# Splitting each weight block once per layer and keeping both parts in HBM scratch

## The chip, the core and the metric

The kernel runs on one core of a Trainium2 chip. The metric is the device time of one execution in microseconds (us). Before the change it is 1161.77 us, the median of three runs (1158.14 to 1165.17).

## The reference

Two layers of a hybrid encoder run over nine tiles of 128 tokens: eight tiles of one prompt of 1024 tokens, and one tile with the 8 x 16 tokens of the sample requests. Both request groups use the same weights. Cut to what matters here:

```
h = x @ w_in                                     # 1024 x 3072
uA, vA, zA, qB, fB, iB, zB, qC, kC, vC, zC = split(h)
yA = sgu(uA, vA) * silu(zA)                      # gated mixing in chunks of 128
yB = norm(hgrn2(qB, fB, iB)) * silu(zB)          # gated recurrence, 4 heads
yC = window_attention(qC, kC, vC) * silu(zC)     # 8 query heads, 2 kv heads
out = layer_norm(alpha * x + concat(yA, yB, yC) @ w_out)   # 1024 x 1024
```

All of it is float32. The outputs are the last layer's rows, the new keys and values, the recurrent states and some normalised rows of the sample.

## The kernel before

**Numbers.** A large product is made of three passes of TensorE (PE) over operands that are each split in a high part (rounded to the format fp32r) and a low part (the remainder): high by high, then the two mixed products, all summed in one PSUM tile (`prod`, L336). So every weight is needed as `wh` and `wl`, and every activation as `xh` and `xl` (or `mixh` and `mixl`).

**Blocks.** The weights are cut in blocks of 1024 x 256: twelve of `w_in` and four of `w_out` per layer, 1 MB each. A block is used for three tiles of tokens. Either it makes three products of 24 matmuls with 256 columns (`tok_major`, L346; the blocks K, Q0, Q1, I, ZB, V and O0 to O3), or two products of 24 matmuls with 384 columns (`feat_major`, L353; F, Q, U, Z, C0, C1).

**Groups.** The nine tiles are worked on in groups of three (`GROUPS`, L45), layer by layer, so there are six groups, n = 0 to 5. Group n runs the twelve `w_in` blocks of its own layer and, between Q1 and the rest, the four `w_out` blocks of group n - 1. The last group's four `w_out` blocks end the program. That makes 96 blocks, and each of the 32 different blocks is loaded and split three times.

**Loading and splitting.** `issue_w` (L274) runs two blocks ahead of the block that PE works on. It takes a pair of buffers `wh`, `wl` (there are two pairs) and issues four loads of 256 KB into staging tiles `wst` (a ring of four; L286). Each loaded piece is then split: ScalarE (ACT) copies it to `wh` with rounding (`copy`, L125), and VectorE (DVE) or GpSimd (POOL) subtracts to get `wl` (`tt`, L142). Which of the two subtracts piece 0 to 3 of a block is read from a table by the block's position in the program:

```
WDVE = ((1, 2), (1, 3), (1, 2, 3), (1,), (1,), (1, 3))
```

Each entry holds for 16 blocks and lists the pieces of DVE; the others are POOL's. The three first blocks go to DVE whole (`WDVE0`). Because a `wh`, `wl` pair is written again two blocks later, the split of a block cannot begin before PE has finished the block two places ahead of it.

**Order of the work.** PE's order is written out by hand (`manual_schedule`): after each product `tick` (L331) puts in a step of the three lanes that do the rest: lane C is attention (L487), lane B the recurrence (`hpre` L608, `lane_b` L654), lane A the gated mixing (L833). The order on ACT, DVE, POOL and on SyncE's (SP) queue is made by a scheduler from priorities. All DMAs are issued on SP, which takes its list in order: a DMA that waits holds up those behind it. Layer norm (`out_norm`, L875) ends in a store of the tile's rows (L900 for layer 0, into the scratch tensor `x1`), and `load_x` (L376, L380) reads them back for the next layer.

Of the kernel before, what the change touches and what calls it, by code (L numbers as in the profile page):

```python
# [8 lines left out]
F32 = mybir.dt.float32  # L9
# [11 lines left out]
P = 128  # L21
CB = 256
# [2 lines left out]
RMS_EPS = 1e-6  # L25
TINY = float(2.0 ** -60)
NWST = 4
WDVE = ((1, 2), (1, 3), (1, 2, 3), (1,), (1,), (1, 3))
NB1 = 3
NC4 = 3  # L30
PPT = 1
# [1 line left out]
WDVE0 = (0, 1, 2, 3)  # L33
# [63 lines left out]
def body(ctx: ExitStack, tc: tile.TileContext, A, O, cst):  # L97
    nc = tc.nc
# [6 lines left out]
    dp = ctx.enter_context(tc.tile_pool(name="dp", bufs=1, space=DRAM))  # L105
# [3 lines left out]
    def T(tag, shape, bufs, dt=F32):  # L109
        uid[0] += 1  # L110
        return sp.tile(shape, dt, tag=tag, bufs=bufs, name=f"{tag}_{uid[0]}")
# [12 lines left out]
    def copy(o, i):  # L124
        return act.activation(o, i, AF.Copy)  # L125
# [3 lines left out]
    def acquire(tag, bufs, *writers):  # L129
        r = rings.setdefault(tag, [0, []])  # L130
        r[0] += 1
        k = r[0] - 1 - bufs
        if k >= 0:
            for w in writers:
                tc.add_manual_dep(w.ins, r[1][k].ins.name, mybir.DependencyInfo(
                    mybir.DependencyClass.NoSync, mybir.DependencyReason.SCHED_ONLY), reason="ring order")

    def release(tag, ins, n=1):
        rings[tag][1] += [ins] * n

    def tt(e, o, a, b, op):
        return e.tensor_tensor(o, a, b, op=op)  # L142
# [125 lines left out]
    wlist += [(order[-1][0], "w_out", cb) for cb in range(4)]  # L268
    wq = []
    wpos = [0]  # L270

    pieces = []

    def issue_w(off=WP):  # L274
        if wpos[0] >= len(wlist):
            return
        l, name, blk = wlist[wpos[0]]
        early = wpos[0] if wpos[0] < NEA else None
        eng_lo = WDVE0 if early is not None else WDVE[min(wpos[0] // 16, 5)]
        wpos[0] += 1  # L280
        with tc.high_priority(offset=off):
            wh, wl = T("wh", [P, 8, CB], 2, F32R), T("wl", [P, 8, CB], 2, F32R)
            for kk in range(4):
                tag, bufs = ("wst", NWST) if early is None or kk == 3 else ("pT", 3) if early % 2 == 0 else ("c4", NC4)
                st = T(tag, [P, 2, CB], bufs)
                ld = nc.sync.dma_start(st, A[name][l, :, blk, 2 * kk:2 * kk + 2, :])  # L286

                def piece(kk=kk, st=st, tag=tag, bufs=bufs, ld=ld):
                    hw, lw = wh[:, 2 * kk:2 * kk + 2, :], wl[:, 2 * kk:2 * kk + 2, :]
                    with tc.high_priority(offset=WP):  # L290
                        copy(hw, st)
                        up = tt(dve if kk in eng_lo else pool, lw, st, hw.bitcast(F32), ALU.subtract)
                    acquire(tag, bufs, ld)
                    release(tag, up)
                pieces.append(piece)
        wq.append((wh, wl))
# [5 lines left out]
    def next_w():  # L302
        do_pieces(99)
        w = wq.pop(0)
        issue_w()
        return w
# [601 lines left out]
    with tc.high_priority(offset=2 * WP):  # L908
        xrs = load_xT(GROUPS[0][:1], 2)
    issue_w(2 * WP - 100)  # L910
    with tc.high_priority(offset=2 * WP - 200):
        xrs += load_xT(GROUPS[0][1:])
# [234 lines left out]
```

## Time and profile before

| | before |
|---|---|
| median of the runs | 1161.77 us |
| the profiled execution | 1161.45 us |
| its span, first to last instruction | 1159.7 us |
| PE busy | 1097.3 us (95%) |
| PE's weight loads busy | 1015.6 us (88%) |
| DVE busy | 833.7 us (72%) |
| ACT busy | 628.6 us (54%) |
| POOL busy | 586.2 us (51%) |
| DMA: bytes, share of the 16 engines | 140.12 MB, 38% |
| mean granted TensorE clock | 0.973 |

The busy time of an engine is the time in which at least one of its instructions ran. Matmuls overlap in the pipeline, so PE's busy time is not its time at full rate. The granted clock is a share of 2.4 GHz. The page of the profile gives sums over the whole span; the windows view gives the same by stretch, and the timeline and the chain of waits tell what an engine stood still for.

### The profile page before, as it was taken

The page shows a single profiled execution, that of the slowest core. Times are in us where ns is not written, and L with a number is a line of the kernel's source. Part 1 is how long each engine was busy: PE and PEld are TensorE (multiplying, and loading weights), DVE is VectorE, ACT ScalarE, POOL GpSimd, SP SyncE. Part 2 cuts the span into 40 slices and gives each one's busy share as a digit, 9 for nine tenths or more (in the row PEclk, how much of TensorE's full clock was granted, in tenths as well). Part 3 has the DMA queues.
Part 4 walks back from the last instruction along what each step waited for, and adds up shares of the span by engine and source line. Part 5 has one row for each costly group of instructions (what it writes and reads, how often), then busy time and mean ns, then how long its engine had stood idle before and what let it go on. Part 6 is the DMA issues. An engine that isn't in the chain of part 4 may idle for free.

```text
span 1159.7 us, 26399 instructions
## 1 busy us (share of the span) xinstructions
PE 1097.3 (95%) x10267; PEld 1015.6 (88%) x10267; DVE 833.7 (72%) x1816; ACT 628.6 (54%) x1533; POOL 586.2 (51%) x634
## 2 busy tenths in 40 slices
PE   9989999999999999989999989999897999989886
PEld 7977799988889988989998978998897999888786
DVE  4688667785786787686777687477749658968965
ACT  5677545665444677444478554465644436554321
POOL 3344374262647235673336765536556461547523
PEclk9999999999999999999999999999999999989998
DMA  9322253253335334325236324324433432443231
GB/s 321 121 74 74 72 157 114 98 179 94 103 112 185 94 119 157 108 75 175 89 100 228 110 75 139 123 92 164 122 101 109 146 119 74 145 146 93 64 99 60
DMA packets 70093, 140.12 MB, mean 121 GB/s; under 512 B 8400, under 2 KB 11984, under 8 KB 69968
## 3 DMA queue, kind: packets, MB, share of 16 engines
q1 hardware_dynamic: 69968, 138.43, 37.7%
q8 instruction: 81, 1.33, 0.5%
q14 instruction: 44, 0.36, 0.1%
HBM read 126.87 MB, written 11.53 MB: 119 GB/s over the span
## 4 chain that ended last, share of the span: by engine, by line
PE 48%; DVE 14%; ACT 3%; POOL 3%; issue 2%; DMA 1%; POOLq 0%; SPq 0%; DVEq 0%; ACTq 0%
PE mm L344 38%; DVE wl L142 2%; PE ax L444 2%; DVE W L142 2%; PE ax L482 2%; PE ax L473 2%; DVE t1b L142 1%; ACT wh L125 1%; POOL sm L369 1%; PE ax L392 1%; POOL X L142 1%; DVE xrow L895 1%; PE ax L844 1%; PE ax L559 1%; DVE AQ L747 1%
## 5 line engine op out<-in xcount | busy, mean ns | idle before, releaser
L142 POOL TENSOR_TENSOR wl<-wst,wh 128x512 fp32r<-128x512 f32 x202 | 291.7, 1462 | 354.0 <-ACT wh L125 215.6
L142 DVE TENSOR_TENSOR wl<-wst,wh 128x512 fp32r<-128x512 f32 x173 | 197.5, 1163 | 116.9 <-ACT wh L125 112.1
L125 ACT ACTIVATE wh<-wst 128x512 fp32r<-128x512 f32 x375 | 206.9, 622 | 107.8 <-PE mm L344 89.5
L344 PE MATMUL mm<-wh,xh 128*128 128x256 f32 x864 | 129.1, 292 | 8.8 <-DVE t3k L364 5.9
L344 PE MATMUL mm<-xh,wh 128*128 128x384 f32 x576 | 127.0, 365 | 2.1 <-DVE t3k L364 1.3
L344 PEld LDWEIGHTS mm<-wh,xh 128*128 128x128 f32 x864 | 112.8, 194 | 14.9 <-DVE t3k L364 6.6
L344 PE MATMUL mm<-wh,xl 128*128 128x256 f32 x864 | 125.0, 288 | 0.0
L344 PE MATMUL mm<-wl,xh 128*128 128x256 f32 x864 | 123.3, 286 | 0.0
L344 PEld LDWEIGHTS mm<-wh,xl 128*128 128x128 f32 x864 | 114.6, 196 | 0.2 <-POOL xl L142 0.2
L344 PE MATMUL mm<-xl,wh 128*128 128x384 f32 x576 | 114.1, 340 | 0.0
L344 PEld LDWEIGHTS mm<-wl,xh 128*128 128x128 f32 x864 | 113.7, 195 | 0.0
L344 PEld LDWEIGHTS mm<-xh,wh 128*128 128x128 f32 x576 | 104.5, 201 | 9.0 <-issue 2.6
L344 PE MATMUL mm<-xh,wl 128*128 128x384 f32 x576 | 111.7, 335 | 0.0
L344 PEld LDWEIGHTS mm<-xl,wh 128*128 128x128 f32 x576 | 104.0, 193 | 0.0
L344 PEld LDWEIGHTS mm<-xh,wl 128*128 128x128 f32 x576 | 101.0, 188 | 0.0
L369 POOL TENSOR_TENSOR sm<-sm,ct 128x4 f32<-128x4 f32 (+2 forms) x42 | 48.7, 1159 | 82.7 <-DVE sm L368 75.6
L344 PE MATMUL mm<-wh,mixh 128*128 128x256 f32 x576 | 85.5, 291 | 4.9 <-ACT mixh L125 4.9
L344 PE MATMUL mm<-wh,mixl 128*128 128x256 f32 x576 | 82.4, 287 | 0.0
L458 ACT ACTIVATE c<-ax,sm 128x256 f32<-128x256 f32 (+1 forms) x128 | 57.4, 460 | 46.1 <-DVE sm L455 42.4
L344 PE MATMUL mm<-wl,mixh 128*128 128x256 f32 x576 | 81.8, 285 | 0.0
L344 PEld LDWEIGHTS mm<-wh,mixh 128*128 128x128 f32 x576 | 74.0, 191 | 5.3 <-ACT mixh L125 5.3
L344 PEld LDWEIGHTS mm<-wh,mixl 128*128 128x128 f32 x576 | 75.9, 196 | 0.0
(212 smaller groups left out, 1948.2 us busy)
## 6 DMA issues: line engine op xcount, KB each, us to landing
wst<-in_w_in SPq DMA_DIRECT2D x279, 256.0 KB, 3.1
wst<-in_w_out SPq DMA_DIRECT2D x96, 256.0 KB, 3.1
xrow<-x SPq DMA_DIRECT2D x18, 512.0 KB, 3.6
x<-xrow SPq DMA_DIRECT2D x9, 512.0 KB, 3.0
xrow<-in_xT SPq DMA_DIRECT2D x8, 512.0 KB, 4.6
xrow<-in_x_prompt SPq DMA_DIRECT2D x8, 512.0 KB, 3.5
out_y_prompt<-xrow SPq DMA_DIRECT2D x5, 512.0 KB, 3.6
pT<-in_w_in SPq DMA_DIRECT2D x6, 256.0 KB, 4.8
```

What stands on the lines that cost most here:

```text
L125: return act.activation(o, i, AF.Copy)
L142: return e.tensor_tensor(o, a, b, op=op)
L344: pe.matmul(out, a(k), b(k), start=n == 0, stop=n == 23)
L369: pool.tensor_tensor(out, out, mh[:, :out.shape[-1]], op=ALU.pow)
L392: pe.transpose(ps[:, k, :], xr[:, (4 * hf + k) * P:(4 * hf + k + 1) * P], idn)
L444: pe.matmul(ps[:, hh, sl], qT[:, hh, 2 * g + j, :], kk, start=hh + c == 0, stop=False)
L458: acquire("c4", NC4, *[act.activation(pt[:, h, sl], pss[h // 2][:, h % 2, sl], AF.Exp, bias=nM[:, h:h + 1], scale=0.125, accum_out=rs[:, h ...
L473: tr = pe.transpose(ps[:, h, :], pt[:, h, b * P:(b + 1) * P], idn)
L482: mm = pe.matmul(pso[64 * u:64 * u + 64], vv[:, g, :], pT[:, u::2, :], start=first, stop=last)
L559: mm = pe.matmul(pso[64 * u:64 * u + 64, b2, g].rearrange("p r i -> p (r i)"), w[:, 2 * p + b2, 64 * g:64 * g + 64], r[:, 64 * g + 32 * u: ...
L747: eng("v").tensor_copy(AQ[o, ch, u::2, :], QG[64 * u:64 * u + 64, :, 64 * ch:64 * ch + 64])
L844: pe.matmul(ps[64 * e:64 * e + 64, tl, :], v3[:, tl, gg * 64:(gg + 1) * 64], d["wsS" if m else "wsP"][:, gg, :], start=True, stop=True)
```

## The change

The first time that a layer's block comes up (groups 0 and 3 for `w_in`, groups 1 and 4 for `w_out`), it is loaded and split as before, and both parts are also written to scratch tensors in HBM, two pieces at a time, in DMAs of 512 KB. The second and third time the parts are read back straight into `wh` and `wl` by four DMAs of 512 KB; nothing is staged or split. The table of DVE's pieces now has one entry per layer: two of the four pieces of every block, after the first three.

```diff
-WDVE = ((1, 2), (1, 3), (1, 2, 3), (1,), (1,), (1, 3))
+WDVE = ((1, 3), (1, 3))
...
+    kept = {}
...
         early = wpos[0] if wpos[0] < NEA else None
-        eng_lo = WDVE0 if early is not None else WDVE[min(wpos[0] // 16, 5)]
+        eng_lo = WDVE0 if early is not None else WDVE[l]
         wpos[0] += 1
+        key = (l, name, blk)
         with tc.high_priority(offset=off):
             wh, wl = T("wh", [P, 8, CB], 2, F32R), T("wl", [P, 8, CB], 2, F32R)
+            if key in kept:
+                for h in range(2):
+                    ks = slice(4 * h, 4 * h + 4)
+                    nc.sync.dma_start(wh[:, ks, :].bitcast(F32), kept[key][0][:, ks, :])
+                    nc.sync.dma_start(wl[:, ks, :].bitcast(F32), kept[key][1][:, ks, :])
+                wq.append((wh, wl))
+                return
+            nm = f"{name}{l}_{blk}"
+            kept[key] = [dp.tile([P, 8, CB], F32, tag=nm + c, name=nm + c) for c in "hl"]
             for kk in range(4):
...
                     with tc.high_priority(offset=WP):
                         copy(hw, st)
                         up = tt(dve if kk in eng_lo else pool, lw, st, hw.bitcast(F32), ALU.subtract)
+                        if kk % 2:
+                            ks = slice(2 * kk - 2, 2 * kk + 2)
+                            nc.sync.dma_start(kept[key][0][:, ks, :], wh[:, ks, :].bitcast(F32))
+                            nc.sync.dma_start(kept[key][1][:, ks, :], wl[:, ks, :].bitcast(F32))
```

In the compiled program ACT's rounding copies fall from 384 to 128, DVE's subtractions for `wl` from 182 to 70, and POOL's from 202 to 58. The DMAs that stage weights fall from 384 to 128, and 128 writes and 256 reads of 512 KB are added. PE's instructions and their order stay as they were.

What moves is shown at three places. The first is SP's queue at the start, where the fourth piece of block I (`wst_372` before, `wst_392` after) waits its turn. `xrow` are the next group's tiles, `lng` and `lnb` the layer norm's parameters. Before:

```order
L286 DMA wst_370<-in_w_in 128x512
L208 DMA xrow_1976<-in_xT 128x1024
L208 DMA xrow_1978<-in_xT 128x1024
L224 DMA lng_2456<-in_ln_g 128x1024
L224 DMA lnb_2458<-in_ln_b 128x1024
L286 DMA wst_372<-in_w_in 128x512
L286 DMA wst_489<-in_w_in 128x512
```

After (`w_in_8h` and `w_in_8l` are the kept parts of block Q1, `w_in_5h` that of I):

```order
L208 DMA xrow_2046<-in_xT 128x1024
L208 DMA xrow_2048<-in_xT 128x1024
L224 DMA lng_2496<-in_ln_g 128x1024
L224 DMA lnb_2498<-in_ln_b 128x1024
L306 DMA w_in_8h<-wh_280 128x1024
L307 DMA w_in_8l<-wl_281 128x1024
L306 DMA w_in_8h<-wh_280 128x1024
L307 DMA w_in_8l<-wl_281 128x1024
L297 DMA wst_392<-in_w_in 128x512
L306 DMA w_in_5h<-wh_382 128x1024
```

The writes of Q1 now stand ahead of the last piece of I; the same four writes for K and for Q0 stand further up.

The second place is SP's queue in group 2, around the end of the `w_out` blocks, where the stores of the normalised rows (`x_91<-xrow`) and the next layer's loads of them lie between the weights of F, Q, U and I. Before, staged pieces:

```order
L286 DMA wst_5756<-in_w_in 128x512
L900 DMA x_91<-xrow_5006 128x1024
L380 DMA xrow_6912<-x_91 128x1024
L286 DMA wst_5850<-in_w_in 128x512
L286 DMA wst_5852<-in_w_in 128x512
```

After, the kept parts (4h is F, 3h is Q, 0h is U, 5h is I):

```order
L289 DMA wl_5403<-w_in_4l 128x1024 x2
L915 DMA x_91<-xrow_4912 128x1024
L288 DMA wh_5604<-w_in_3h 128x1024 x2
L289 DMA wl_5605<-w_in_3l 128x1024 x2
L395 DMA xrow_6676<-x_91 128x1024
L915 DMA x_91<-xrow_4914 128x1024
L915 DMA x_91<-xrow_4916 128x1024
L395 DMA xrow_6678<-x_91 128x1024
L288 DMA wh_5692<-w_in_0h 128x1024 x2
```

The reads of a block stand behind the stores of the rows and wait in the same queue for PE to release the buffer.

The third place is ACT's list at the end, from the last products of C1 (`tanh`) to the last layer norm. Before:

```order
L362 ACTIVATE tanh_14473<-mm_14448 128x384
L125 ACTIVATE mixh<-oT_12458 128x384
L125 ACTIVATE mixh<-u_1767_13196 128x384
L125 ACTIVATE wh_14543<-wst_14545 128x512
L125 ACTIVATE wh_14543<-wst_14547 128x512
L125 ACTIVATE wh_14543<-wst_14551 128x512
L125 ACTIVATE wh_14543<-wst_14549 128x512
L362 ACTIVATE tanh_14517<-mm_14492 128x384
```

After:

```order
L377 ACTIVATE tanh_13941<-mm_13916 128x384
L125 ACTIVATE mixh<-oT_12076 128x384
L125 ACTIVATE mixh<-u_1559_12766 128x384
L377 ACTIVATE tanh_13983<-mm_13958 128x384
L125 ACTIVATE mixh<-ax_13989 128x2x128
```

The four copies ahead of the last `tanh` are gone, as are the two subtractions ahead of its user on DVE.

## Rows read from the trace of the kernel before

**Rows 1.** The page's busy times: engine, us (share of the span), instructions.

```profile
PE 1097.3 (95%) x10267; PEld 1015.6 (88%) x10267; DVE 833.7 (72%) x1816; ACT 628.6 (54%) x1533; POOL 586.2 (51%) x634
```

**Rows 2.** Windows, groups 0 to 5, last four blocks: length, busy PE PEld DVE ACT POOL, clock, DMA, GB/s.

```profile
0.00:157.40 157.40, 145.91 (x1315) 130.65 (x1316) 107.51 (x265) 102.88 (x252) 69.34 (x85) 0.97 0.41 130
157.40:351.20 193.80, 186.84 (x1850) 172.26 (x1849) 144.93 (x312) 104.18 (x265) 93.93 (x98) 0.98 0.40 127
351.20:533.80 182.60, 178.73 (x1655) 166.19 (x1655) 131.45 (x279) 107.63 (x256) 97.22 (x121) 0.99 0.40 124
533.80:720.70 186.90, 179.22 (x1640) 167.35 (x1639) 137.41 (x294) 108.25 (x265) 100.12 (x94) 0.97 0.40 126
720.70:918.90 198.20, 189.43 (x1876) 175.90 (x1875) 135.16 (x302) 101.94 (x260) 108.54 (x116) 0.97 0.39 122
918.90:1108.40 189.50, 180.54 (x1656) 167.21 (x1655) 148.43 (x318) 94.04 (x223) 100.13 (x110) 0.97 0.35 111
1108.40:1150.00 41.60, 36.67 (x291) 36.10 (x289) 23.83 (x42) 8.53 (x17) 11.93 (x10) 0.96 0.19 61
```

**Rows 3.** Windows, same columns: a packed stretch, and one in which DMA is full.

```profile
400.00:440.00 40.00, 40.00 (x304) 35.90 (x303) 32.12 (x68) 31.59 (x90) 10.85 (x7) 1.00 0.38 130
...
24.00:26.00 2.00, 2.00 (x19) 2.00 (x18) 0.27 (x1) 0.38 (x1) 0.00 (x0) 1.00 1.02 417
```

**Rows 4.** Waits of PE: instruction, who it waited for, us in total, times, longest.

```profile
PE ax L827 <- DVE t1b L142: 16.6, 11, 2.9
PE mm L344 <- DVE t3k L364: 7.2, 5, 3.1
PE mm L344 <- ACT mixh L125: 4.9, 1, 4.9
...
PE mm L344 <- ACT wh L125: 1.5, 2, 1.3
```

**Rows 5.** The page's groups: the split; busy us, mean ns, idle before, releaser.

```profile
L142 POOL TENSOR_TENSOR wl<-wst,wh 128x512 fp32r<-128x512 f32 x202 | 291.7, 1462 | 354.0 <-ACT wh L125 215.6
L142 DVE TENSOR_TENSOR wl<-wst,wh 128x512 fp32r<-128x512 f32 x173 | 197.5, 1163 | 116.9 <-ACT wh L125 112.1
L125 ACT ACTIVATE wh<-wst 128x512 fp32r<-128x512 f32 x375 | 206.9, 622 | 107.8 <-PE mm L344 89.5
```

**Rows 6.** Timeline of POOL and DVE in group 4: start, us, instruction, count.

```profile
820.50 4.13 POOL L142 TENSOR_TENSOR wl<-wst,wh 128x512 fp32r<-128x512 f32 x3
...
887.47 0.89 DVE L142 TENSOR_TENSOR X<-X,t3k 128x128 f32<-128x128 f32 x4
```

**Rows 7.** The chain of waits in group 4 and at the first block of group 2.

```profile
821.98 3.76 DVE X L142 x5
...
351.49 8.62 PE mm L344 x72
```

**Rows 8.** Timeline at the last product of C1: ACT, DVE and PE.

```profile
1108.60 2.18 ACT L125 ACTIVATE wh<-wst 128x512 fp32r<-128x512 f32 x4
...
1109.77 3.02 DVE L142 TENSOR_TENSOR wl<-wst,wh 128x512 fp32r<-128x512 f32 x2 [0.48 <-ACT wh L125]
...
1114.66 0.58 PE L344 MATMUL mm<-wh,mixh 128*128 128x256 f32 x1 [4.93 <-ACT mixh L125]
```

**Rows 9.** DMA issues: form, count, KB each, median us from issue to landing.

```profile
xrow<-x SPq DMA_DIRECT2D x18, 512.0 KB, 3.6
x<-xrow SPq DMA_DIRECT2D x9, 512.0 KB, 3.0
```

**Rows 10.** Timeline of block I in group 0: its last split, and PE's start.

```profile
33.02 0.62 ACT L125 ACTIVATE wh<-wst 128x512 fp32r<-128x512 f32 x1
...
35.42 1.12 PE L344 MATMUL mm<-wh,xh 128*128 128x256 f32 x8
```

**Rows 11.** Timeline in group 2: a store on SP, and PE's start of block F.

```profile
425.56 0.33 SPq L900 DMA_DIRECT2D x<-xrow  x1
...
430.75 1.66 PE L344 MATMUL mm<-xh,wh 128*128 128x384 f32 x8
```

## The prediction

> **What bounds the kernel now.** I read the page's busy times first. PE is busy 1097.3 of 1159.7 us, the next engine 833.7 [rows 1]. So the question is how much of the remaining 62.4 us the change can reach. The windows tell where that is [rows 2]: PE's busy time falls short of the stretch by 11.5 us in group 0, 7.0, 3.9, 7.7, 8.8 and 9.0 us in groups 1 to 5, and 4.9 us in the last four blocks; most of the rest is the last layer norm. The same rows give the granted clock, 0.96 to 0.99 of full speed, so a little PE time is also lost to stretches at the lower of its two levels (1.2 and 2.4 GHz).
>
> That busy PE is really full shows in a packed stretch of attention and output blocks [rows 3]: 40 us of 40 at clock 1.00, no idle time at all, with PE's weight loads at 35.9 us, 90%. The Trainium skill ("Trainium Kernel Development and Optimization", Performance Expectations) says that matmul busy time is a bad metric and weight-load busy share a good one. By that share, 88%, some 12% or 140 us would be open; the packed row, where nothing is open at 90%, does not bear that out.
>
> What PE waits for is mostly not the weights. The direct wait for a rounded weight is 1.5 us in all; the long ones are results of DVE (t1b 16.6 us, t3k 7.2) and one of ACT (mixh 4.9) [rows 4]. These engines carry the split in their lists: 291.7 us on POOL, 197.5 on DVE, 206.9 on ACT, and the subtractions stand idle in the list besides, for 354.0 and 116.9 us, until a copy is done or PE releases the buffer [rows 5]. Whatever stands behind them waits too. So the split costs PE time by making the lanes late.
>
> **What the change takes away.** 64 of 96 blocks are read instead of split: 256 copies on ACT by 0.55 us (206.9/375) are 141 us, 112 subtractions on DVE by 1.163 are 130 us, 144 on POOL by 1.462 are 211 us [rows 5]. Nearly all of it leaves groups 1, 2, 4, 5 and the end. In these four groups DVE is busy 560 of 764 us and POOL 400 [rows 2]; about 123 and 202 us of that go, so DVE falls from 73% to 57% and POOL from 52% to 26%. DVE's other work also gets faster: while POOL ran three subtractions in 4.13 us, five small multiplications took DVE 3.76 us in the chain, 0.75 each; away from such pieces four of them took 0.89, 0.22 each [rows 6, 7].
>
> What can be won is bounded by PE's missing time there: 7.0 + 3.9 + 8.8 + 9.0 = 28.7 us, 4.9 us at the end, and the clock's share, (1 - clock) times the stretch, 3.9 + 1.8 + 5.9 + 5.7 + 1.7 = 19 us [rows 2]. Part of the lower clock lies in the idle time itself, so the ceiling is about 50 us. I take two thirds, 33 us: a queue's waits go about as busy over idle, 0.73/0.27 = 2.7 now and 0.57/0.43 = 1.3 after, which halves them, and the shorter operations beside POOL add to it. One place can be followed exactly. At the last product of C1 ACT does four copies (2.18 us) and DVE two subtractions (3.02 us) ahead of that product's own evacuation, and PE stands 4.93 us until mixh is there [rows 8]; with them gone some 4 us go. What is late next are the lanes' own chains, which is the third that I leave. Bounds: 17 us (only a third, the chains dominate) and 50.
>
> **What it adds at the start.** Each of the 32 split blocks writes 2.1 MB. In SP's order the fourth piece of block I now stands behind the twelve writes of K, Q0 and Q1, 6.29 MB. In the trace the queue is full then: 417 GB/s at share 1.02 [rows 3], so the writes push the piece back by 6.29/417 = 15.1 us. It was split at 33.02 us; now at about 48.1. PE starts I at 35.42 us and reaches the piece's rows with its seventh matmul of about 0.12 us, near 36.1 [rows 10]. That is a stall of about 12.5 us with the copy's 0.6; I take 12. The upper bound is the mean rate per share of group 0, 130/0.41 = 317 GB/s [rows 2]: 19.8 us, a stall of 17. The lower bound is 4: the lanes catch up meanwhile, and most of group 0's 11.5 us may be saved again. Behind I the order repeats (writes of a block, loads of the next), 3.1 MB per block or 7.5 us at 417 GB/s, under the 8.62 us that PE needs for a bare block [rows 7], so I put the rest of groups 0 and 3 at nothing; if the rate falls to 317 it is 9.9 us and each bare block there costs a little over 1. Twelve more of group 3's pieces go to DVE and twelve fewer to POOL; PE's idle time there is 7.7 us [rows 2], and I take 0 with bounds of 4 either way. A write waits on SP for its copy and its subtraction; behind it stand staging loads that wait for the same subtractions to free `wst`, so that wait is not new.
>
> **What the reads cost.** A read cannot start before PE releases the pair two blocks back, so it has the stay of one block on PE: 8.62 us at least [rows 7], 764/64 = 11.9 in the mean [rows 2]. One DMA of 512 KB lands 3.6 us after issue [rows 9]; three more at 417 GB/s take 1.26 us each, so a block is there after 7.4 us, and its first half, which is all that the first matmuls want, after less. That is hidden with 1.2 us to spare. The cover goes if the rate falls to 317 GB/s (8.6 us), or if SP is held. For the second I looked at the stores between the reads: in group 2 the first was issued at 425.56, and block F began on PE at 430.75 [rows 11], so the store is out of the queue at about the time that the next buffer is released. I take 0, with 20 us as the upper bound (two blocks of three tight ones in each of four groups late by 2 us, and the lower clock after each).
>
> **Sum.** Against the profiled execution's own 1161.45 us (0.3 under the median): -33 + 12 = -21, so 1140 us.
>
> **Rivals.** (a) The lanes' own chains are the limit and only 17 us come back: 1161.5 - 17 + 12 = 1156. For it: the direct waits on the split are small [rows 4]. Against: the slowed operations of rows 6 and 7, and the end of rows 8.
>
> (b) Slower: the reads come late. Before, staging ran a block ahead of the buffer; now one DMA stream must land within one block's stay. If a block takes 12 us to land (250 GB/s, 8.4 us, and a hold on SP), the half of the 64 blocks whose window lies between 8.62 and 11.9 us is late by 1.7 us in the mean, 54 us: 1161.5 + 54 + 12 - 33 = 1194. It decides from about 10.7 us on: with windows spread evenly from 8.62 to about 15 us, 64 x 2.1/6.4 = 21 blocks are then late by 1 us in the mean, which eats the net gain. For it: traffic grows from 140 to 274 MB. Against: 417 GB/s seen, and a mean share of only 0.35 to 0.41 per group [rows 2, 3]. The Trainium skill ("SBUF — State Buffer", the section on a bandwidth-pool intuition that's wrong) says that HBM is almost always the end-to-end bottleneck; by that rule the added 134 MB would come out on the span, at 417 GB/s some 320 us, and the shares of rows 2 say that it isn't so here.
>
> (c) Everything that PE misses comes back and the start is mostly absorbed: 1161.5 - 50 + 4 = 1115. For it: rows 6 to 8. Against: long chains of small operations in lane B stay.
>
> **Chances.** Forecast 0.58 (its own range 1126 to 1153), (a) 0.17, (b) 0.14, (c) 0.11. The range that leaves out two in ten goes from 1115, which takes in (c)'s point, to 1162, which takes in (a) and the upper bounds of start and reads. A measurement of this kernel can tell about 0.5% (6 us) from no change. Faster by more: the forecast, (c) and a third of (a), 0.74. Within it: most of (a), 0.10. Slower: (b) and the worst of (a), 0.16.
>
> **What would show it.** Right: ACT's copies near 70 us, DVE's subtractions near 80 and POOL's near 85; PE's idle time in groups 1, 2, 4, 5 together down from 28.7 to about 10 us; a wait of PE for the last piece of I near 36 us, about 12 us long; no wait of PE for a read of kept parts beyond 1 us; DMA share about 0.7. Wrong: PE waiting for DMAs into `wh` in block after block, which is (b); or the same t1b and t3k waits with DVE at 57%, which is (a).

## The result, and the profile after

The changed kernel takes 1126.71 us (median of four runs, 1125.85 to 1127.15); the kernel before took 1159.95 us beside it (1153.80 to 1165.17). The ratio is 0.9714, with a 95% interval of 0.9664 to 0.9765. The profiled execution of the change took 1125.85 us, with a span of 1124.1 us.

The page's busy times of the change, in the form of [rows 1]:

```profile
PE 1080.9 (96%) x10267; PEld 1003.2 (89%) x10267; DVE 652.5 (58%) x1704; ACT 503.8 (45%) x1277; POOL 367.8 (33%) x490
```

DVE lost 181 us, POOL 218 and ACT 125, while PE's instructions are the same. Of DVE's 181 us 136 are subtractions of the split (197.5 in [rows 5], 61.5 in the groups below); the other 45 come from operations that are the same in number and got shorter. Where it counts is seen in the windows by group (the columns of [rows 2]; the bounds are where the same products begin):

```profile
0.00:174.00 174.00, 149.73 (x1314) 135.49 (x1315) 100.92 (x263) 101.55 (x247) 65.56 (x83) 0.90 0.78 270
174.00:356.10 182.10, 181.96 (x1851) 168.71 (x1850) 106.86 (x289) 79.74 (x215) 56.09 (x73) 1.00 0.70 248
356.10:533.80 177.70, 176.98 (x1657) 164.57 (x1655) 91.59 (x234) 79.32 (x199) 65.93 (x105) 1.00 0.64 228
533.80:718.20 184.40, 177.57 (x1641) 165.58 (x1638) 122.94 (x295) 98.34 (x243) 71.21 (x73) 0.98 0.79 282
718.20:902.80 184.60, 184.48 (x1877) 171.40 (x1874) 108.94 (x295) 78.10 (x212) 51.59 (x75) 1.00 0.68 239
902.80:1077.90 175.10, 175.10 (x1656) 162.78 (x1654) 101.71 (x289) 63.61 (x160) 49.14 (x75) 1.00 0.63 216
1077.90:1114.30 36.40, 34.92 (x291) 34.63 (x288) 14.50 (x34) 1.89 (x4) 3.17 (x4) 1.00 0.53 183
```

Against the lengths in [rows 2], group 0 became 16.6 us longer, groups 1 to 5 became 11.7, 4.9, 2.5, 13.6 and 14.4 us shorter, and the last blocks 5.2: +16.6 - 52.3 = -35.7, which is the difference of the two spans (35.6). Groups 1, 2, 4 and 5 and the last blocks, where the prediction puts the relief, make 49.8 of the 52.3 us. In groups 1, 2, 4 and 5 PE now misses 0.14, 0.72, 0.12 and 0.00 us, 1.0 in all where it missed 28.7, and the granted clock there is 1.00. Group 3, which splits and writes like group 0, is 2.5 us shorter all the same.

The page's groups of what is left of the split, in the form of [rows 5]:

```profile
L142 POOL TENSOR_TENSOR wl<-wst,wh 128x512 fp32r<-128x512 f32 x58 | 84.6, 1472 | 210.2 <-ACT wh L125 126.2
L142 DVE TENSOR_TENSOR wl<-wst,wh 128x512 fp32r<-128x512 f32 x61 | 61.5, 1015 | 67.1 <-ACT wh L125 52.7
L125 ACT ACTIVATE wh<-wst 128x512 fp32r<-128x512 f32 x119 | 69.5, 625 | 34.3 <-DMA wst<-in_w_in 19.0
```

And the waits of PE, in the form of [rows 4], the four longest:

```profile
PE mm L359 <- ACT wh L125: 16.0, 4, 13.1
PE ax L842 <- DVE t1b L142: 4.2, 2, 3.0
PE ax L497 <- ACT pT L125: 2.6, 1, 2.6
PE ax L701 <- ACT kvt L125: 2.5, 1, 2.5
```

The waits for t1b fell from 16.6 to 4.2 us, those for t3k (7.2) are gone from the list, and mixh at the end of C1 went from 4.9 to 1.5. A new wait heads the list: 13.1 us for one `wh`. The timeline of PE, ACT and SP shows it (start, us, instruction; in brackets the idle time before it and who ended it):

```profile
38.27 0.33 SPq L297 DMA_DIRECT2D wst<-in_w_in  x1
```

```profile
48.49 0.63 ACT L125 ACTIVATE wh<-wst 128x512 fp32r<-128x512 f32 x1 [12.76 <-DMA wst<-in_w_in]
```

```profile
35.15 0.88 PE L359 MATMUL mm<-wh,xh 128*128 128x256 f32 x6
49.18 0.80 PE L359 MATMUL mm<-wh,xh 128*128 128x256 f32 x2 [13.15 <-ACT wh L125]
49.77 1.91 PE L359 MATMUL mm<-wh,xl 128*128 128x256 f32 x8
```

This is block I: after six of the first eight matmuls PE stands until the fourth piece is split, at 48.49 us instead of 33.02 [rows 10]. Its load left SP at 38.27 us, behind the writes of K, Q0 and Q1. After the stall eight matmuls take 1.91 us instead of 1.12. In two windows over the stall, with the same columns, the DMA engines are full, and while PE stands the clock falls to half, its lower level:

```profile
34.00:38.00 4.00, 2.03 (x17) 1.82 (x16) 3.77 (x7) 0.80 (x2) 2.08 (x2) 1.00 1.04 409
38.00:48.00 10.00, 0.00 (x0) 0.00 (x0) 0.00 (x0) 0.00 (x0) 0.00 (x0) 0.51 1.03 391
```

The reads cost PE nothing: no wait for a kept part is in its list. They are not as quick as the prediction had them, though. The DMA issues (form, count, KB, median us to landing) and SP's timeline at two blocks in group 2:

```profile
wh<-w_in_9h SPq DMA_DIRECT2D x8, 512.0 KB, 5.1
wl<-w_in_9l SPq DMA_DIRECT2D x8, 512.0 KB, 7.6
```

```profile
364.06 0.80 SPq L288 DMA_DIRECT2D wh<-w_in_8h  x2
365.02 1.12 SPq L289 DMA_DIRECT2D wl<-w_in_8l  x2
...
372.70 0.80 SPq L288 DMA_DIRECT2D wh<-w_out_0h  x2
```

Over all reads the high halves land 3.8 to 7.6 us after issue (median 5.0), the low ones 5.3 to 9.9 (median 7.0), and the low ones are issued 1 us later. So a block is complete some 8 us after its first read, in a window of 8.64 us (372.70 - 364.06) between bare blocks; only the low part is close, and PE asks for it last: by the kernel's order of matmuls, in the third eight of a product.

### The profile page after: what moved, and what is told of

It is laid out like the page before. It is cut to its first block, busy times and chain, and to the rows that moved or that the text cites. A ratio compares the mean times of both kernels' runs of the same rounds, so it can differ in the third digit from the quotient of the medians.

```text
span 1124.1 us, 25834 instructions
## 1 busy us (share of the span) xinstructions
PE 1080.9 (96%) x10267; PEld 1003.2 (89%) x10267; DVE 652.5 (58%) x1704; ACT 503.8 (45%) x1277; POOL 367.8 (33%) x490
## 5 line engine op out<-in xcount | busy, mean ns | idle before, releaser
L142 POOL TENSOR_TENSOR wl<-wst,wh 128x512 fp32r<-128x512 f32 x58 | 84.6, 1472 | 210.2 <-ACT wh L125 126.2
L359 PE MATMUL mm<-xh,wh 128*128 128x384 f32 x576 | 121.4, 353 | 0.0
L359 PEld LDWEIGHTS mm<-xh,wh 128*128 128x128 f32 x576 | 99.5, 192 | 5.9 <-issue 2.9
L142 DVE TENSOR_TENSOR wl<-wst,wh 128x512 fp32r<-128x512 f32 x61 | 61.5, 1015 | 67.1 <-ACT wh L125 52.7
L125 ACT ACTIVATE wh<-wst 128x512 fp32r<-128x512 f32 x119 | 69.5, 625 | 34.3 <-DMA wst<-in_w_in 19.0
L359 PEld LDWEIGHTS mm<-wl,mixh 128*128 128x128 f32 x576 | 74.3, 192 | 0.0
```

The costliest lines, as they stand in the source:

```text
L359: pe.matmul(out, a(k), b(k), start=n == 0, stop=n == 23)
```

## The experiments

Each ran beside the kernel before on one chip. Times are medians, ratios are to the kernel before. Its medians were 1159.95 to 1162.58 us in these comparisons, so a difference of under 3 us to the change's 1126.71 us tells nothing.

**1. The writes of the start moved.** K, Q0 and Q1 are not written when they are first split, but split a second time in group 1 and written then.

```diff
-            kept[key] = [dp.tile([P, 8, CB], F32, tag=nm + c, name=nm + c) for c in "hl"]
+            first = early is None
+            if first:
+                kept[key] = [dp.tile([P, 8, CB], F32, tag=nm + c, name=nm + c) for c in "hl"]
...
-                        if kk % 2:
+                        if first and kk % 2:
```

> The three first blocks (K, Q0, Q1 of layer 0) are split in group 0 without being written; group 1 splits them again and writes them then. Theory: the 13.15 us for which PE stands at the last piece of block I come from the 6.29 MB of writes ahead of that piece in SP's queue; without them PE waits there under 1 us, group 0 is back from 174 to about 158 us, and the time is about 1112 us (1108 to 1116), 1 or 2 us being paid for the second split in group 1. Rival: the piece is late for another reason (SP held by the copies that a write waits for, or a slower queue as such), and the time stays at 1122 to 1127 us.

Measured: 1108.59 us (1107.70 to 1109.81), ratio 0.9549 (0.952 to 0.9578). The waits of PE for a rounded weight, the window of the first 160 us, and PE's first matmuls of group 1, which begins in it:

```profile
PE mm L361 <- ACT wh L125: 2.3, 3, 1.2
```

```profile
0.00:160.00 160.00, 146.48 (x1348) 132.17 (x1349) 105.07 (x271) 106.18 (x258) 71.84 (x87) 0.99 0.77 263
```

```profile
156.03 1.12 PE L361 MATMUL mm<-wh,xh 128*128 128x256 f32 x8
```

The stall is gone, the clock of this stretch is 0.99 instead of 0.90, and group 0 ends at 156.0 us instead of 174.0. So the 18.1 us that separate this run from the change lie in group 0 and come from the writes ahead of block I's load; the three more splits in group 1 cost hardly anything. The run takes away the writes' bytes and their waits on SP together. The trace of the change tells them apart: up to 38.3 us, when that load leaves, SP waits 0.6 us for a copy and 0.7 us for a subtraction, and nearly all of its other waits there are for transfers to land. So the rival's hold by the copies is small, and the full queue is the cause. This version is 4.5% faster than the kernel before and the best of this study.

**2. The table alone.** The kernel before with the new table of DVE's pieces.

```diff
-WDVE = ((1, 2), (1, 3), (1, 2, 3), (1,), (1,), (1, 3))
+WDVE = ((1, 3), (1, 3))
...
-        eng_lo = WDVE0 if early is not None else WDVE[min(wpos[0] // 16, 5)]
+        eng_lo = WDVE0 if early is not None else WDVE[l]
```

> The kernel before with the new table of DVE's pieces only: every block is still split three times. Theory: the table is worth nothing by itself, 1155 to 1165 us. Rival: the more even sharing of the subtractions between DVE and POOL is a part of the gain, then 1140 to 1150 us.

Measured: 1163.91 us (1159.01 to 1168.21), ratio 1.0018 (0.9999 to 1.0037). The table is worth nothing by itself.

**3. The writes alone.** Every block is split each time as before, with the new table; the first split is written, nothing is read back.

```diff
-            if key in kept:
+            if False:
...
+            first = key not in kept
...
-                        if kk % 2:
+                        if first and kk % 2:
```

> The changed kernel with the writes to scratch but no reads: every block is split three times, and written the first time. Theory: the writes cost only at the start (13 us of stall and 2 us of lower clock), so 1160 + 15 = 1175 us (1170 to 1182), and PE's idle time in groups 1 to 5 is that of before. Rival: the writes also hold SP's queue for the staging loads of group 3, then 1185 us and more; or they cost nothing with the split engines as slow as before, then 1160 us.

Measured: 1181.48 us (1179.01 to 1185.12), ratio 1.0173 (1.0128 to 1.0217). The writes cost 18.9 us against the kernel before beside this run, and the wait at the start is in the waits of PE again, beside those of the kernel before:

```profile
PE ax L844 <- DVE t1b L142: 19.8, 11, 3.4
PE mm L361 <- ACT wh L125: 16.8, 4, 14.6
PE mm L361 <- ACT mixh L125: 4.9, 1, 4.9
```

Theory held; its range ended at 1182. So the reads in place of the split are worth 1181.5 - 1126.7 = 54.8 us: the relief by a second way, near the 52.3 us of the windows.

**4. ACT's copies stay.** A block read back brings only its low part; the source is loaded and copied to `wh` by ACT again.

```diff
-                    nc.sync.dma_start(wh[:, ks, :].bitcast(F32), kept[key][0][:, ks, :])
                     nc.sync.dma_start(wl[:, ks, :].bitcast(F32), kept[key][1][:, ks, :])
+                for kk in range(4):
...
+                            up = copy(wh[:, 2 * kk:2 * kk + 2, :], st)
```

> The second and third time only the low part is read back; the high part is made again by ACT's copies from staged pieces. So DVE and POOL are relieved as in the change and ACT is not; the bytes moved are the same. Theory: the waits that went were DVE's and POOL's, so the time is within 6 us of the change, 1127 to 1133 us. Rival: ACT's copies and their waits for PE were what made the lanes late, then 1140 to 1155 us.

Measured: 1131.68 us (1130.34 to 1136.20), ratio 0.9754 (0.9719 to 0.9789). The page of this run has ACT as busy as before the change, and DVE and POOL as after it:

```profile
PE 1080.4 (96%) x10267; PEld 1001.4 (89%) x10267; DVE 658.6 (58%) x1704; ACT 632.8 (56%) x1533; POOL 368.8 (33%) x490
```

The 256 copies were worth 5 us of the 54.8. The rest belongs to DVE and POOL.

**5 and 6. Half of the low parts made again, on POOL or on DVE.** Of each block read back two of four low pieces are not read but loaded as source and subtracted again, on POOL (pieces 0 and 2) or on DVE (1 and 3).

```diff
+                for kk in range(4):
+                    ps = slice(2 * kk, 2 * kk + 2)
+                    if kk % 2 != 0:
+                        nc.sync.dma_start(wl[:, ps, :].bitcast(F32), kept[key][1][:, ps, :])
+                        continue
+                    st = T("wst", [P, 2, CB], NWST)
+                    ld = nc.sync.dma_start(st, A[name][l, :, blk, ps, :])
...
+                            up = tt(pool, wl[:, ps, :], st, wh[:, ps, :].bitcast(F32), ALU.subtract)
```

> In blocks that are read back, POOL makes two of the four low pieces again (from staged pieces and the high part that was read); the other two and the high part are read. POOL has 186 subtractions (202 before, 58 after the change), DVE 70 and ACT 128 copies as in the change; the bytes moved are the same. Theory: POOL's subtractions count most, since they stretch DVE's operations beside them, so about two thirds of the relief is lost: 1140 to 1152 us. Rival: DVE's own subtractions count most, then at most 1137 us here.

> The same with DVE instead of POOL: DVE has 198 subtractions (182 before, 70 after the change), POOL 58. Theory (POOL's count most): about a third of the relief is lost, 1132 to 1142 us, and less than with POOL. Rival (DVE's count most): 1142 to 1155 us, more than with POOL.

Measured: POOL 1154.86 us (1152.67 to 1157.58), ratio 0.9954 (0.9938 to 0.9970); DVE 1157.90 us (1152.57 to 1163.39), ratio 0.9966 (0.9943 to 0.9988). That is 28.2 and 31.2 us over the change, where I had expected about two thirds and one third of the gain. Read from the other end: against the run with the writes alone, where POOL and DVE both make two of four, taking DVE's half away (and ACT's copies) is worth 26.6 us, taking POOL's half away (and the copies) 23.6, and both together 54.8. The halves add up only roughly: counted from the change they make 59.4 us and counted from the writes alone 50.2, with ACT's 5 us twice in it. But each engine holds about one half. Both times lie above the ranges of theory and of rival, and the 3 us between them tell nothing; so neither engine counts more than the other.

What the two runs look like, busy times of the POOL run and then of the DVE run:

```profile
PE 1088.7 (94%) x10267; PEld 1008.7 (87%) x10267; DVE 703.2 (61%) x1704; ACT 500.6 (43%) x1277; POOL 534.2 (46%) x618
```

```profile
PE 1089.0 (94%) x10267; PEld 1007.7 (87%) x10267; DVE 736.6 (64%) x1832; ACT 499.4 (43%) x1277; POOL 378.7 (33%) x490
```

No engine is near full, and PE's waits behind the stall at the start are short ones (t1b 8.7 and 6.6 us in all): some 28 us are lost in many places. The subtraction itself is not what PE waits for. A remade low part comes between a landing and PE's use, but in the POOL run PE has one wait for a low part of POOL's in all, 1.3 us long, and the change itself has one of 1.2:

```profile
PE mm L372 <- POOL wl L142: 1.3, 1, 1.3
```

In the POOL run DVE is busy 51 us longer with the same 1704 instructions. Four of DVE's groups tell how, first in the change, then in the POOL run:

```profile
L142 DVE TENSOR_TENSOR X<-X,t3k 128x128 f32<-128x128 f32 x124 | 34.4, 339 | 5.6 <-ACT X L656 5.3
L762 DVE COPY AQ<-EG 64x128 f32<-64x128 f32 x64 | 22.6, 353 | 6.5 <-ACT AQ L125 5.0 <-PE ax L826 0.2
L885 DVE BATCH_NORM_STATS2 lst<-xrow 128x6 f32<-128x256 f32 x72 | 30.6, 425 | 1.8
L1003 DVE TENSOR_TENSOR_SCAN t3k<-mab,t3k 128x128 f32<-128x128 bf16 x36 | 12.5, 416 | 5.2 <-ACT t3k L999 5.2
```

```profile
L142 DVE TENSOR_TENSOR X<-X,t3k 128x128 f32<-128x128 f32 x124 | 41.7, 401 | 4.9 <-ACT X L669 4.6
L775 DVE COPY AQ<-EG 64x128 f32<-64x128 f32 x64 | 25.5, 398 | 7.2 <-ACT AQ L125 6.0
L898 DVE BATCH_NORM_STATS2 lst<-xrow 128x6 f32<-128x256 f32 x72 | 30.6, 425 | 1.8
L1016 DVE TENSOR_TENSOR_SCAN t3k<-mab,t3k 128x128 f32<-128x128 bf16 x36 | 17.7, 559 | 5.2 <-ACT t3k L1012 5.2
```

Operations of DVE with two operands in SBUF (X and the scan) got 18% and 34% longer beside POOL's subtractions; the statistics, with one, kept their 425 ns. But the copies to AQ have one operand too and got 13% longer, so the number of operands alone does not decide. The Trainium skill ("SBUF — State Buffer", Who interferes with whom) has this rule: a VectorE instruction with two SBUF inputs contends with a GpSimd one that reads SBUF; one with at most one does not, unless it runs in a 2-port mode, which a copy can. The rows of X, the scan and the statistics agree with it; that the copies ran in such a mode is not shown here.

**7. The low part read twice.** Each low half of a kept block is read two times, 3.1 MB per block.

```diff
                     nc.sync.dma_start(wl[:, ks, :].bitcast(F32), kept[key][1][:, ks, :])
+                    nc.sync.dma_start(wl[:, ks, :].bitcast(F32), kept[key][1][:, ks, :])
```

> The changed kernel with the low part of each read block read twice, one DMA after the other: 3.1 MB per block instead of 2.1, 67 MB more in all. Theory: a block then takes 2.3 + 3.1/0.417 = 9.9 us to land, longer than the shortest stay of a block on PE (8.62 us) but shorter than the mean (11.9), and the low part is wanted 2 us later than the high part: 0 to 10 us more than the change, with waits of PE for DMA only at K, Q0 and Q1. Rival (the reads were at the edge already): 25 us more and over, with waits of PE for DMA in most blocks.

Measured: 1243.79 us (1239.05 to 1248.91), ratio 1.0729 (1.068 to 1.0778), 117 us over the change. Theory (0 to 10 us) missed, and the time is on the rival's side. PE waits for kept parts now, 63.2 us in 33 waits, all for low parts (two rows of them here); and SP waits too:

```profile
PE mm L360 <- DMA wl<-w_in_0l: 14.1, 6, 4.7
PE mm L360 <- DMA wl<-w_in_8l: 12.1, 3, 4.9
```

```profile
SPq L290 <- DMA wl<-w_in_11l: 34.1, 8, 8.2
SPq L290 <- DMA wl<-w_out_3l: 33.6, 8, 7.7
```

SP's rows show a flaw of this run: the second read writes the buffer that the first one writes, so it waits on SP until the first has landed, and holds the next block's reads behind it. The run therefore stretches a block's reads more than its bytes do, and at 275 GB/s in groups 1 and 2 it does not show what traffic alone would cost. What it does show is that the reads have an edge: when a block takes about twice as long to be there, 64 blocks lose 1.8 us each in the mean.

**8 to 11. Work and wait apart.** Is it the work of a subtraction that delays the lanes, or the subtraction's wait in the list, behind which everything else stands? Two runs give DVE or POOL, for each block read back, the work without a wait: ten subtractions of constants of 128x104. Two others give the wait without the work: two subtractions of two columns whose inputs are the landed parts.

```diff
+                            for _ in range(5):
+                                up = tt(dve, dum, ct[:, 0:104], ct[:, 104:208], ALU.subtract)
```

```diff
+                            tt(dve, dum[:, 0:2], wl[:, k, 0:2].bitcast(F32), wh[:, k, 0:2].bitcast(F32), ALU.subtract)
```

> For each of the 64 blocks read back VectorE gets ten subtractions of two constants of 128x104 (about the work of two 128x512 subtractions, 2.0 to 2.9 us a block), placed in its list where the remade low parts stood, but waiting for no transfer and no buffer. The run in which VectorE remade two low parts of each block took 1157.9 us, the change 1126.7. Theory (it is the hold: an instruction that waits in the list for a landed part keeps what is behind it): the work without the wait costs little, 1127 to 1136 us. Rival (it is the work itself that makes the chains of the lanes late): 1148 to 1160 us, with waits of TensorE for t1b, AQ and c as in that run.

> The same ten subtractions of constants for each block on GpSimd, without a wait. The run in which GpSimd remade two low parts of each block took 1154.9 us. Theory (hold): 1127 to 1136 us. Rival (work, on GpSimd or by what it takes from VectorE): 1146 to 1158 us.

> The wait without the work: for each block read back VectorE gets two subtractions of two columns only, whose inputs are the landed high and low part of that block's halves, in the places of the remade low parts. Theory (hold): most of the 31 us of the run with the whole subtractions comes back, 1143 to 1160 us. Rival (work): at most 5 us over the change, 1126 to 1132 us.

> The same two short subtractions that wait for the landed parts, on GpSimd. Theory (hold): most of the 28 us of the run with GpSimd's whole subtractions, 1141 to 1157 us. Rival (work): 1126 to 1132 us.

Measured, and against the change's 1126.71: DVE's work 1145.27 us (1143.02 to 1147.36), +18.6; DVE's wait 1135.69 (1134.04 to 1137.09), +9.0; POOL's work 1135.95 (1134.67 to 1137.95), +9.2; POOL's wait 1127.16 (1126.38 to 1128.22), +0.4. The ratios are 0.9853 (0.983 to 0.9875), 0.9770 (0.9751 to 0.9789), 0.9774 (0.9754 to 0.9794) and 0.9695 (0.9675 to 0.9714). The added groups, one row from each run in the order of the times just given:

```profile
L142 DVE TENSOR_TENSOR dum<-ct 128x104 f32<-128x104 f32 x640 | 199.7, 312 | 10.8
```

```profile
L142 DVE TENSOR_TENSOR dum<-wl,wh 128x2 f32<-128x2 f32 x128 | 27.8, 217 | 159.6 <-DMA wl<-w_in_8l 33.2
```

```profile
L142 POOL TENSOR_TENSOR dum<-ct 128x104 f32<-128x104 f32 x640 | 290.1, 453 | 42.5
```

```profile
L142 POOL TENSOR_TENSOR dum<-wl,wh 128x2 f32<-128x2 f32 x128 | 31.3, 244 | 394.7 <-DMA wl<-w_in_4l 46.5
```

Theory and rival both fall as single causes. On DVE both parts count, 18.6 + 9.0 = 27.6 of the 31.2 us; the short pieces are 200 us of work, where the whole subtractions had added 95 (156.4 - 61.5), so twice the work stands behind the 18.6 us, in pieces of a third of the length; the sum is a fit, not a proof. DVE's run also had staged source parts, for which SP waited 168.6 us until DVE freed a buffer; what that cost was not tested. On POOL 395 us of waiting in the list cost nothing that can be told from noise, and 290 us of work in short pieces 9; 18.6 of the 28.2 us were left open.

**12. POOL's whole subtractions without the staging.** The low part lands as in the change, and POOL subtracts zero from two of its four pieces in place.

```diff
+                    nc.sync.dma_start(wl[:, ps, :].bitcast(F32), kept[key][1][:, ps, :])
+                    if kk % 2 != 0:
+                        continue
...
+                            tt(pool, wl[:, ps, :], wl[:, ps, :].bitcast(F32), zero.unsqueeze(2).to_broadcast([P, 2, CB]), ALU.subtract)
```

> As the run in which GpSimd remade two of four low parts of each block read back (1154.9 us), with the same transfers in bytes, but GpSimd's whole 128x512 subtractions take the landed low part itself less zero, in place, so that nothing goes through the staging buffers wst. GpSimd's work in ten short pieces without a wait cost 9 us (1136.0), its wait without the work nothing (1127.2). Theory (the length of one instruction counts: 1.4 us whole, beside or ahead of a lane's step, delays more than ten short ones): 1147 to 1157 us, with VectorE's busy time above 690 us. Rival (the missing 19 us came from the source parts going through wst again, whose buffers hold SP): 1132 to 1140 us, VectorE at 680 us.

Measured: 1144.39 us (1143.67 to 1145.12), ratio 0.9846 (0.983 to 0.9863), 17.7 us over the change and 10.5 under the run with the subtractions made again. It lies between theory and rival (DVE's busy time, 690.9 us, is where theory put it): whole instructions, which here also wait in the list, cost about twice what short ones did, and the rest is gone without the staged source parts. For the second SP's waits have a row, first of run 5, then of this one:

```profile
SPq L295 <- POOL wl L142: 277.9, 110, 6.4
SPq L288 <- PE mm L372: 144.2, 51, 8.9
```

```profile
SPq L290 <- PE mm L370: 330.0, 61, 15.2
```

With the source parts staged, the DMA queue stands 277.9 us for POOL to free a staging buffer; here it waits for PE to release the weight buffers, as it does in the change. That this wait is the cause of the 10.5 us was not shown; POOL's pieces were also shorter here (1089 ns against 1379), with a single column as one operand, and DVE was busy 12 us less than in run 5 (690.9 against 703.2), which is a second candidate.

## Why the prediction was right, and where its sizes were off

It said 1140 us, faster, in a range of 1115 to 1162; 1126.7 is inside the range, just above the lower end of the forecast's own (1126 to 1153), and a little nearer to rival (c)'s 1115 than to the 1140. The two terms of its sum are the two that the traces show: a relief of the lanes and a stall at the start. Their sizes were off in opposite directions, 17 us too little relief and 4.6 us too short a start, so that part of the closeness is luck.

**What bounds the kernel.** Right. PE is busy 96% of the span, and what changed is how much of groups 1, 2, 4 and 5 it misses. The waits that went are those of [rows 4] for DVE's results, and the engines' work came out about as counted: 84.6 us of POOL's subtractions (about 85 said), 69.5 of copies and 5.5 more for the nine from other staging buffers (about 70), and 61.5 of DVE's subtractions and 7.2 more for such nine (about 80), since one takes 1015 ns in the mean instead of 1163. That DVE's operations get shorter was said too, but from two places with 0.75 and 0.22 us per multiplication; in the mean of all 124 of these (X<-X,t3k) it is 400 ns before and 339 after.

**The relief, -33 us (17 to 50).** The step that was off is "I take two thirds". All of the ceiling of about 50 us came back: 49.8 us by the windows of groups 1, 2, 4, 5 and the end, and 54.8, group 3 included, by the run with the writes alone. The ceiling itself, PE's missing time in those groups and at the end and the share of the clock, was right: 28.7 us of idle time became 1.0, where the prediction's sign was about 10, and the clock 1.00. The reason for two thirds was that a queue's waits go about as busy over idle and so would halve; DVE at 58% to 59% in groups 1, 4 and 5 leaves PE with 0.3 us of idle time in the three. Nor does the loss go by busy time: in run 8 DVE is busy 70% of the span (805.0 us) and 18.6 us are lost, in run 5 it is 61% and 28.2 are. The third that I left to the lanes' own chains does not exist here.

That the price hangs on the engines' lists was argued from [rows 5] for all three; runs 4 to 6 show it for DVE and POOL and hardly for ACT (5 us). Each half of the low work holds about half of the relief. How is less sure: on DVE the work itself and the wait in its list count (runs 8 and 10), with the staging untested; on POOL whole instructions count, and the staging or longer pieces beside DVE (runs 9, 11 and 12). The idle time ahead of POOL's subtractions, 354.0 us in [rows 5], was read as a hold of what is behind. In the changed kernel's list 395 us of it cost 0.4; in the busier list of the kernel before it was not tried.

**The start, +12 us (4 to 17).** Right in mechanism and place: the fourth piece of I was split at 48.49 us (48.1 said), and PE stood 13.15 us for it from about 36.0 (12 to 12.5 from near 36.1 said). Missed was what follows a stall: the clock at half when PE resumes, 1.91 us for eight matmuls, a clock of 0.90 over group 0, and so 16.6 us for the group. With the writes moved the gain was 18.1. Rival (c), in which the start is mostly absorbed, had the relief right and this part wrong.

**The rest of groups 0 and 3, 0.** About right: group 3 has its writes and got 2.5 us shorter, at a DMA share of 0.79. The table counts for nothing (run 2).

**The reads, 0.** Right in the result, not in the margin. The 7.4 us came from one DMA's 3.6 us [rows 9] and 417 GB/s; the reads of a block take about 8 us, at 305 to 349 GB/s where I looked in group 2 (windows of 366 to 372 us). Rival (b) stood nearer than its 0.14 was argued from: its tipping point, 10.7 us, is less than 3 us above what a block takes, and run 7 went over it. What saves the reads is probably that the parts land in the order in which the products use them; no run changed that order.

**The rivals.** (a) needed t1b and t3k waits to stay at DVE's 57%; they went. The Trainium skill's rule that stands with (b) ("SBUF — State Buffer", A bandwidth-pool intuition that's wrong), HBM as the end-to-end bottleneck almost always, is not borne out here: 134 MB more were moved and the groups' DMA shares rose to 0.63 to 0.79, but of PE's waits only the one at the start, where the share was 1.03, is for a transfer in a full queue.

## What to carry to other kernels

Work that an engine does for the main engine's operands costs more than its direct waits show, because it stands among steps of other chains in the same list: here 1.5 us of direct waits stood for more than 50 us. Bound such a relief by what the main engine misses, its clock included. The busy share of the other engines does not tell how much of it comes: with DVE at 58% all of it came, in run 5 at 61% half of it was lost, in run 8 at 70% a third. When a value is kept for later use, look at what the store is queued ahead of; not storing the first three blocks, at the cost of splitting them once more, gave another 18 us.

## What the runs showed that I had not expected

- POOL can wait in its list for 395 us and its work can come in short pieces of 453 ns, 290 us in all, at 0.4 and 9.2 us of time; 128 whole pieces of 1089 ns, 139 us in all, cost 17.7. Less work cost more. The whole pieces also hold a wait, and the low part lands in four DMAs instead of two, so length alone is not separated from that. PE itself waited for POOL's low parts only 1.3 us in all.
- DVE's wait without work cost 9.0 us with 27.8 us of instructions, POOL's 0.4. A likely reason, not tested, is that more of the results that PE waits for come from DVE.
- A stall of 13.15 us cost 16.6 to 18.1: the clock was at 0.51 while PE stood, and the next sixteen matmuls ran at 1.91 us per eight.
